# A softmax with a relative bias: the first chunk loaded in two halves, the second half shared unevenly among the DMA engines

## The chip, the cores and the metric

The kernel runs on one core of a Trainium2 chip. The metric is the device time of one execution in microseconds. Three runs of the kernel before gave a median of 1329.82 us (1329.43 to 1330.29). A profile was taken of one execution, and the views quoted here are answers of its trace.

## What is computed

The reference adds a bias to attention logits and takes a softmax over the last axis. The bias depends on the head and on the distance of the two positions, clipped to 16 on either side:

```python
B, H, S, max_rel = 2, 8, 2112, 16
rel = pos[:, None] - pos[None, :]                    # pos = 0 .. S-1
bias = rel_bias[:, clip(rel, -16, 16) + 16]          # rel_bias: (8, 33)
x = logits + bias[None]                              # logits: (2, 8, 2112, 2112) float32
x = exp(x - x.max(-1)); out = x / x.sum(-1)
```

Input and output have 285 MB each, so 571 MB pass through the core; the bias table has 264 numbers.

## The kernel before, in words

The 33,792 rows of 2,112 numbers are dealt out to the 128 partitions: partition p has 264 rows that follow one another in memory, and eight partitions share a head. The work goes in 44 chunks of six rows per partition. A chunk is 128 x 12,672 numbers, 6.49 MB. Four buffers X0 to X3 (`NBUF`) hold chunks; chunk n uses buffer n mod 4, and is loaded, computed on in place, and stored from there.

Before the loop, the bias table is brought to all partitions (line 97, the queue of ScalarE) into the first 264 columns of a tile F, on every partition all eight heads. VectorE makes masks from two index patterns that GpSimd writes (lines 117 to 128), keeps the row of the partition's own head by a multiplication and a sum over heads (lines 131 and 135, into `rbS`), and from it writes a long strip M of bias values into PSUM (lines 138 to 155). For every four chunks (24 rows) the stretch of M that these rows need is copied to F (line 160), so F is used twice: for the table first, then for the strips.

Per chunk, VectorE adds the bias to each row and finds the row's extreme in one instruction (line 166, six to a chunk), ScalarE takes the exponential and its sum (line 175), and VectorE scales by the reciprocal (lines 183 and 187), three rows at a time. Semaphores link them: `ld[b]` tells VectorE that chunk b has landed, `added` and `expd` link VectorE and ScalarE row by row, and `scaled` tells SP that rows are ready to be stored. A wait followed by a decrement is the helper `take` (line 74), and so many waits stand under L74.

All large transfers are issued by SP, in an order written out by hand. First come the loads of the first four chunks: chunk 0 as six transfers of one row per partition (line 88), the other three whole (line 78). Then the loop (line 204): store a chunk once it is scaled (line 82), wait until the store before it has landed (`st[b]`), and load the next chunk into the buffer that this has freed. The last chunk is stored in two halves of three rows. VectorE begins the loop when the first five transfers of chunk 0 have landed (`pre`, line 190), copies the strip, and then waits for `ld[0]`, the sixth.

A transfer of a tile of 128 partitions is cut into 128 packets, one per partition, which 16 DMA engines carry, eight each: a packet is 8,448 B for one row, 25,344 B for three rows, 50,688 B for a whole chunk. Each engine works through its own packets in the order of their issue. A DMA's semaphore rises by 16 in all.

Of the kernel before, what the change touches and what calls it, by code (L numbers as in the profile page):

```python
# [15 lines left out]
def kernel(  # L16
# [6 lines left out]
    nc = tc.nc  # L23
    P = 128
    B, H, S, S2 = logits.shape
    assert S == S2
    MR = 16
    W = 2 * MR + 1
    ROWS = B * H * S // P
    PB = S // ROWS  # L30
    assert ROWS * P == B * H * S and PB * ROWS == S and PB == H == 8
    R = 6
    NBUF = 4
    STEP = R * NBUF
    N = ROWS // R
    HALF = R // 2
    assert ROWS % STEP == 0
    MW = S + ROWS - 1
    FW = S + STEP - 1
    BIG = 3.0e38  # L40

    io = ctx.enter_context(tc.tile_pool(name="io", bufs=1))
    X = [io.tile([P, R * S], FP32, tag=f"X{b}", name=f"X{b}") for b in range(NBUF)]
    F = io.tile([P, FW], FP32, tag="F", name="F")
    rbS = io.tile([P, W], FP32, tag="rbS", name="rbS")
# [3 lines left out]
    ip = io.tile([P, 3, PB], I32, tag="ip", name="ip")  # L49
# [3 lines left out]
    def view(t, offset, dims):  # L53

        return bass.AP(tensor=t.tensor, offset=t.offset + offset, ap=[[list(t.ap[0])[0], P]] + dims)

    def rows(t, j, n):

        return bass.AP(tensor=t.tensor, offset=t.offset + j * S, ap=[[ROWS * S, P], [1, n * S]])

    with tc.tile_critical(no_gpsimd_drain=True):
        ld = [nc.alloc_semaphore(f"ld{b}") for b in range(NBUF)]
# [3 lines left out]
        scaled = nc.alloc_semaphore("scaled")  # L66
        inv = nc.alloc_semaphore("inv")
        rb = nc.alloc_semaphore("rb")
        pre = nc.alloc_semaphore("pre")
        idx = nc.alloc_semaphore("idx")  # L70
        dve = nc.alloc_semaphore("dve")

        def take(eng, sem, n):
            eng.wait_ge(sem, n).then_inc(sem, -n)  # L74


        def load(j, b):
            nc.sync.dma_start(out=X[b][:, :], in_=rows(logits, j, R)).then_inc(ld[b], 16)
# [5 lines left out]
            ).then_inc(st[b], 16)  # L84


        for r in range(R):
            nc.sync.dma_start(
                out=X[0][:, r * S : (r + 1) * S], in_=rows(logits, r, 1)
            ).then_inc(ld[0] if r == R - 1 else pre, 16)  # L90
        for n in range(1, NBUF):
            load(n * R, n)

        rbB = view(F, 0, [[1, H * W]])
        nc.scalar.dma_start(
            out=rbB,
            in_=bass.AP(tensor=rel_bias.tensor, offset=rel_bias.offset, ap=[[0, P], [1, H * W]]),
        ).then_inc(rb, 16)  # L100
        nc.gpsimd.iota(ip[:, 0], pattern=[[0, PB]], base=0, channel_multiplier=1).then_inc(idx, 1)
        nc.gpsimd.iota(ip[:, 2], pattern=[[1, PB]], base=0, channel_multiplier=0).then_inc(idx, 1)  # L102

        v = nc.vector
        done = [0]

        def then(ins):
            done[0] += 1
            ins.then_inc(dve, 1)

        def settle():
            v.wait_ge(dve, done[0])

        SC = H * W
        mask = [F[:, SC + i * PB : SC + (i + 1) * PB] for i in range(9)]
        dp, dh, eq, hm, gt, le, lt, ra, rz = mask
        v.wait_ge(idx, 2)
        then(v.tensor_scalar(out=ip[:, 1], in0=ip[:, 0], scalar1=3, scalar2=7,  # L118
                             op0=ALU.logical_shift_right, op1=ALU.bitwise_and))
# [7 lines left out]
        for m, op in ((eq, ALU.is_equal), (gt, ALU.is_gt), (le, ALU.is_le), (lt, ALU.is_lt)):  # L127
# [4 lines left out]
            out=view(F, 0, [[W, H], [1, W]]), in0=view(F, 0, [[W, H], [1, W]]),  # L132
            in1=view(F, SC + 3 * PB, [[1, H], [0, W]]), op=ALU.mult))
        settle()
        then(v.tensor_reduce(out=rbS[:, :], in_=view(F, 0, [[1, W], [W, H]]),  # L135
                             axis=mybir.AxisListType.X, op=ALU.add))
        settle()
        low, high = rbS[:, W - 1 : W], rbS[:, 0:1]
        then(v.tensor_scalar(out=ra, in0=gt, scalar1=low, scalar2=None, op0=ALU.mult))  # L139
        then(v.tensor_scalar(out=rz, in0=gt, scalar1=low, scalar2=None, op0=ALU.mult))  # L140
        then(v.tensor_tensor(  # L141
            out=view(F, 0, [[W, PB], [1, W]]), in0=view(F, SC + 2 * PB, [[1, PB], [0, W]]),
            in1=view(rbS, W - 1, [[0, PB], [-1, W]]), op=ALU.mult))
# [6 lines left out]
            out=view(M, U, [[ROWS, PB], [1, W]]), in0=view(F, 0, [[W, PB], [1, W]]),  # L150
            in1=view(F, SC + 8 * PB, [[1, PB], [0, W]]), op=ALU.add))
        then(v.tensor_copy(out=view(M, U + W, [[ROWS, PB], [1, ROWS - W]]),  # L152
                           in_=view(F, SC + 7 * PB, [[1, PB], [0, ROWS - W]])))
        then(v.tensor_copy(out=M[:, 0:U], in_=low.to_broadcast([P, U])))  # L154
# [7 lines left out]
        def add(b):  # L162
            take(v, ld[b], 16)
            for r in range(b * R, (b + 1) * R):
                x = X[b][:, (r - b * R) * S : (r - b * R + 1) * S]
                v.tensor_tensor_reduce(  # L166
                    out=x, in0=x, in1=F[:, STEP - 1 - r : STEP - 1 - r + S], scale=-1.0, scalar=BIG,
                    op0=ALU.add, op1=ALU.min, accum_out=nmax[:, r : r + 1],
# [18 lines left out]
                    v.tensor_scalar_mul(out=x, in0=x, scalar1=rec[:, r : r + 1]).then_inc(scaled, 1)  # L187

        v.sem_inc(dve, -done[0])
        take(v, pre, 16 * (R - 1))  # L190
        with nc.Fori(0, ROWS - STEP + 1, STEP, engines=[ENG.DVE]) as j:  # L191
            strip(j)
            take(v, dve, 1)
# [51 lines left out]
```

## Time and profile before

| what | value |
|---|---|
| median of three runs | 1329.82 us (1329.43 to 1330.29) |
| span of the profiled execution | 1327.7 us |
| VectorE busy | 976.6 us (74%) |
| ScalarE busy | 575.2 us (43%) |
| DMA | 571.11 MB, mean 430 GB/s |
| SP's queue (q1) | 13,536 packets, 99.6% of 16 engines' span |
| bias table (q10) | 0.14 MB, lands 6.2 us after its issue |

The profile's span runs from the program's first instruction to its last, and so the profiled execution's own time is known as this span of 1327.7 us; it is 2.1 us below the median of the runs, which are timed as a whole. In the page, busy times are per engine, a digit is a fortieth of the span, and the GB/s are what the 16 DMA engines moved together. A view of windows gives for each stretch its length, the busy time of VectorE (DVE), ScalarE (ACT) and GpSimd (POOL) with the number of instructions, TensorE's clock, the mean busy share of the DMA engines, and GB/s; packets are counted in the window in which they start, so that a share can be over 1. In a timeline a row has start, length, engine, line, operation and operands; a bracket gives the idle time before it and what ended it. An engine's name with a q is its queue of instructions that only issue or wait.

### The profile page before, as it was taken

Reading aid. Unit: us, or ns where it says so; the run is one execution under the profiler, and the core shown is the slowest. Engines: PE = TensorE matmul, PEld = TensorE weight load, DVE = VectorE, ACT = ScalarE, POOL = GpSimd, SP = SyncE. Lnnn points to the kernel's source line nnn. Section 1 sums busy time; section 2 is a strip of 40 time slices with the busy share of each in tenths; the row PEclk is TensorE's granted clock in tenths of the full one; section 3 lists DMA queues with packets and bytes.
Section 4 is the critical chain, followed back from the end, with each engine's and each line's share of the span. In section 5 each row is a group of like instructions: output and inputs, shape, how many; then the busy total and the mean of one; then the engine's idle time right before and its main releaser. Section 6 shows DMA issues by size and latency. Waiting matters only on the chain. (4 is left out here: it accounts for less than half of the span.)

```text
span 1327.7 us, 2454 instructions
## 1 busy us (share of the span) xinstructions
DVE 976.6 (74%) x911; ACT 575.2 (43%) x539; POOL 0.4 (0%) x6
## 2 busy tenths in 40 slices
DVE  6999667777777776687778777677877776687772
ACT  2564333444444343345444333444444343335440
POOL 0000000000000000000000000000000000000000
DMA  9999999999999999999999999999999999999998
GB/s 392 431 428 437 435 420 437 435 434 425 435 437 434 428 435 434 435 429 429 438 438 432 426 438 437 437 425 437 437 437 425 435 440 437 428 432 438 437 426 359
DMA packets 13683, 571.11 MB, mean 430 GB/s; under 512 B 1521, under 2 KB 1649, under 8 KB 1649
## 3 DMA queue, kind: packets, MB, share of 16 engines
q1 hardware_dynamic: 13536, 570.96, 99.6%
q10 hardware_dynamic: 144, 0.14, 0.1%
q14 instruction: 3, 0.02, 0.0%
HBM read 285.61 MB, written 285.47 MB: 430 GB/s over the span
## 5 line engine op out<-in xcount | busy, mean ns | idle before, releaser
L166 DVE CUSTOM_DVE_ANT_0 X<-X,F 128x2112 f32<-128x2112 f32 x264 | 605.2, 2354 | 301.3 <-DVEq L74 301.3
L175 ACT ACTIVATE X<-X,nmax 128x2112 f32<-128x2112 f32 x264 | 541.7, 2052 | 539.3 <-ACTq L74 517.6
L187 DVE TENSOR_SCALAR X<-X,rec 128x2112 f32<-128x2112 f32 x264 | 332.4, 1315 | 13.2
L175 ACT ACT_TABLE_LOAD x11 | 14.1, 1283 | 183.3 <-ACTq L74 183.3
L175 ACT ACTIVATION_READ_ACCUMULATOR X<-X,nmax 128x1 f32 x264 | 49.2, 186 | 0.0
L160 DVE COPY F<-M 128x2135 f32 x11 | 26.1, 2374 | 6.3 <-DVEq L74 6.3
L166 DVE DVE_READ_ACCUMULATOR2_ANT nmax<- 128x1 f32 x264 | 21.7, 82 | 0.0
L183 DVE RECIPROCAL rec<-tot 128x3 f32<-128x3 f32 x88 | 14.9, 170 | 0.0
L131 DVE TENSOR_TENSOR F<-F 128x264 f32<-128x264 f32 x1 | 0.4, 434 | 4.7 <-DMA F<-in_rel_bias_dram 4.7
L152 DVE COPY M<-F 128x1848 f32<-128x1848 f32 x1 | 2.1, 2077 | 0.0
L118 DVE TENSOR_SCALAR ip<-ip 128x8 int32<-128x8 int32 x1 | 0.2, 173 | 1.3 <-POOL ip L102 1.3
L135 DVE TENSOR_REDUCE rbS<-F 128x33 f32<-128x264 f32 x1 | 0.6, 610 | 0.0
L149 DVE TENSOR_TENSOR M<-F 128x264 f32<-128x264 f32 x1 | 0.4, 441 | 0.0
L141 DVE TENSOR_TENSOR F<-F,rbS 128x264 f32<-128x264 f32 x1 | 0.4, 425 | 0.0
L128 DVE TENSOR_SCALAR F<-F 128x8 f32<-128x8 f32 x4 | 0.4, 166 | 0.0
L154 DVE COPY M<-rbS 128x247 f32<-128x247 f32 x1 | 0.4, 408 | 0.0
L139 DVE TENSOR_SCALAR F<-F,rbS 128x8 f32<-128x8 f32 x1 | 0.2, 231 | 0.0
L145 DVE SCALAR_TENSOR_TENSOR F<-F,rbS 128x8 f32<-128x8 f32 x1 | 0.2, 225 | 0.0
L140 DVE TENSOR_SCALAR F<-F,rbS 128x8 f32<-128x8 f32 x1 | 0.2, 222 | 0.0
L146 DVE SCALAR_TENSOR_TENSOR F<-F,rbS 128x8 f32<-128x8 f32 x1 | 0.2, 219 | 0.0
L124 DVE TENSOR_TENSOR F<-ip 128x8 f32<-128x8 int32 x1 | 0.2, 167 | 0.0
L121 DVE TENSOR_TENSOR F<-ip 128x8 f32<-128x8 int32 x1 | 0.2, 166 | 0.0
(9 smaller groups left out, 1.2 us busy)
## 6 DMA issues: line engine op xcount, KB each, us to landing
X<-in_logits_dram SPq DMA_DIRECT2D x43, 6336.0 KB, 44.6
out_dram<-X SPq DMA_DIRECT2D x43, 6336.0 KB, 52.6
X<-in_logits_dram SPq DMA_DIRECT2D x6, 1056.0 KB, 12.1
out_dram<-X SPq DMA_DIRECT2D x2, 3168.0 KB, 21.1
F<-in_rel_bias_dram ACTq DMA_DIRECT2D x1, 132.0 KB, 6.2
```

Of the source, the lines that this page charges most:

```text
L128: then(v.tensor_scalar(out=m, in0=dp, scalar1=0.0, scalar2=None, op0=op))
L131: then(v.tensor_tensor(out=view(F, 0, [[W, H], [1, W]]), in0=view(F, 0, [[W, H], [1, W]]), in1=view(F, SC + 3 * PB, [[1, H], [0, W]]), op= ...
L135: then(v.tensor_reduce(out=rbS[:, :], in_=view(F, 0, [[1, W], [W, H]]), axis=mybir.AxisListType.X, op=ALU.add))
L141: then(v.tensor_tensor(out=view(F, 0, [[W, PB], [1, W]]), in0=view(F, SC + 2 * PB, [[1, PB], [0, W]]), in1=view(rbS, W - 1, [[0, PB], [-1, ...
L149: then(v.tensor_tensor(out=view(M, U, [[ROWS, PB], [1, W]]), in0=view(F, 0, [[W, PB], [1, W]]), in1=view(F, SC + 8 * PB, [[1, PB], [0, W]] ...
L152: then(v.tensor_copy(out=view(M, U + W, [[ROWS, PB], [1, ROWS - W]]), in_=view(F, SC + 7 * PB, [[1, PB], [0, ROWS - W]])))
L154: then(v.tensor_copy(out=M[:, 0:U], in_=low.to_broadcast([P, U])))
L160: v.tensor_copy(out=F[:, :], in_=M[:, bass.ds(ROWS - STEP - j, FW)]).then_inc(dve, 1)
L166: v.tensor_tensor_reduce(out=x, in0=x, in1=F[:, STEP - 1 - r : STEP - 1 - r + S], scale=-1.0, scalar=BIG, op0=ALU.add, op1=ALU.min, accum_ ...
L175: nc.scalar.activation(out=x, in_=x, func=EXP, scale=-1.0, bias=nmax[:, r : r + 1], accum_out=tot[:, r : r + 1],).then_inc(expd, 1)
L183: v.reciprocal(out=rec[:, r0 : r0 + HALF], in_=tot[:, r0 : r0 + HALF]).then_inc(inv, 1)
L187: v.tensor_scalar_mul(out=x, in0=x, scalar1=rec[:, r : r + 1]).then_inc(scaled, 1)
```

## The change

Three things are changed, all of them before the loop; the loop itself is the same.

- Chunk 0 is loaded in two halves of three rows per partition. The first half is one transfer of 128 packets of 25,344 B. The second half is cut by partitions into eight transfers (`FAN`) of 64, 16, 13, 11, 9, 7, 5 and 3 partitions. The 64 are the even partitions, the 16 are every eighth from 1 on; the lanes 3, 5 and 7 of each group of eight are cut in pairs, 13 and 3, 11 and 5, 9 and 7 partitions. If a transfer of k partitions (k of 16 or fewer) goes to the same first k engines, one packet each, the engines carry 11, 11, 11, 10, 10, 9, 9, 8, 8, 7, 7, 6, 6, 5, 5 and 5 of the packets of the second half.
- The bias table is brought to 16 partitions (every eighth) and no longer to all 128. VectorE first fills the 264 columns with zeros; ScalarE's queue waits for that before it issues the transfer. Behind the sum over heads, two 32 x 32 transposes with a copy between them spread a partition's row over its group of eight, and a copy puts it into `rbS`.
- VectorE begins the loop when both `pre` (the first half) and `fan` (seven of the eight transfers) have come; the eighth raises `ld[0]`.

```diff
+    GROUPS = P // 16
+    FAN = [(64, 0, 0, 2), (16, 0, 1, GROUPS)]
+    FAN += [(k, 0, lane, GROUPS) for lane, k in ((3, 13), (5, 11), (7, 9))]
+    FAN += [(16 - k, k, lane, GROUPS) for k, _, lane, _ in FAN[:1:-1]]
...
-        for r in range(R):
-            nc.sync.dma_start(
-                out=X[0][:, r * S : (r + 1) * S], in_=rows(logits, r, 1)
-            ).then_inc(ld[0] if r == R - 1 else pre, 16)
...
-        rbB = view(F, 0, [[1, H * W]])
-        nc.scalar.dma_start(
-            out=rbB,
-            in_=bass.AP(tensor=rel_bias.tensor, offset=rel_bias.offset, ap=[[0, P], [1, H * W]]),
-        ).then_inc(rb, 16)
...
+        then(v.memset(F[:, 0 : H * W], 0.0))
+
+        nc.scalar.wait_ge(dve, 1)
+        nc.scalar.dma_start(
+            out=bass.AP(tensor=F.tensor, offset=F.offset, ap=[[PB * list(F.ap[0])[0], P // PB], [1, H * W]]),
+            in_=bass.AP(
+                tensor=rel_bias.tensor, offset=rel_bias.offset, ap=[[0, P // PB], [1, H * W]]
+            ),
+        ).then_inc(rb, 16)
+        nc.sync.dma_start(out=X[0][:, 0 : HALF * S], in_=rows(logits, 0, HALF)).then_inc(pre, 16)
+        PSX = list(X[0].ap[0])[0]
+        for i, (k, g, lane, step) in enumerate(FAN):
+            p = g * GROUPS + lane
+            nc.sync.dma_start(
+                out=bass.AP(
+                    tensor=X[0].tensor, offset=X[0].offset + p * PSX + HALF * S,
+                    ap=[[step * PSX, k], [1, HALF * S]],
+                ),
+                in_=bass.AP(
+                    tensor=logits.tensor, offset=logits.offset + (p * ROWS + HALF) * S,
+                    ap=[[step * ROWS * S, k], [1, HALF * S]],
+                ),
+            ).then_inc(ld[0] if i == len(FAN) - 1 else fan, 16)
...
+        Q = 32
+        RB, RT, RC, RW = [SC + 9 * PB + 2 * Q * i for i in range(4)]
+        then(v.memset(F[:, RB : RB + 2 * Q], 0.0))
...
-        then(v.tensor_reduce(out=rbS[:, :], in_=view(F, 0, [[1, W], [W, H]]),
+        then(v.tensor_reduce(out=F[:, RB : RB + W], in_=view(F, 0, [[1, W], [W, H]]),
                              axis=mybir.AxisListType.X, op=ALU.add))
+        settle()
+        then(v.transpose(out=F[:, RT : RT + 2 * Q], in_=F[:, RB : RB + 2 * Q]))
+        settle()
+        then(v.tensor_copy(out=view(F, RC, [[Q, 2], [PB, Q // PB], [1, PB]]),
+                           in_=view(F, RT, [[Q, 2], [PB, Q // PB], [0, PB]])))
+        settle()
+        then(v.transpose(out=F[:, RW : RW + 2 * Q], in_=F[:, RC : RC + 2 * Q]))
+        settle()
+        then(v.tensor_copy(out=rbS[:, :], in_=F[:, RW : RW + W]))
...
-        take(v, pre, 16 * (R - 1))
+        take(v, pre, 16)
+        take(v, fan, 16 * (len(FAN) - 1))
```

More of the change, by code (lines that the diff above doesn't have):

```diff
@@ L40 @@
     BIG = 3.0e38
+    GROUPS = P // 16
+    FAN = [(64, 0, 0, 2), (16, 0, 1, GROUPS)]
+    FAN += [(k, 0, lane, GROUPS) for lane, k in ((3, 13), (5, 11), (7, 9))]
+    FAN += [(16 - k, k, lane, GROUPS) for k, _, lane, _ in FAN[:1:-1]]
+    assert sum(k for k, _, _, _ in FAN) == P
     io = ctx.enter_context(tc.tile_pool(name="io", bufs=1))
@@ L68 @@
         rb = nc.alloc_semaphore("rb")
-        pre = nc.alloc_semaphore("pre")
         idx = nc.alloc_semaphore("idx")
         dve = nc.alloc_semaphore("dve")
+        pre = nc.alloc_semaphore("pre")
+        fan = nc.alloc_semaphore("fan")
         def take(eng, sem, n):
@@ L84, in store @@
             ).then_inc(st[b], 16)
-        for r in range(R):
-            nc.sync.dma_start(
-                out=X[0][:, r * S : (r + 1) * S], in_=rows(logits, r, 1)
-            ).then_inc(ld[0] if r == R - 1 else pre, 16)
-        for n in range(1, NBUF):
-            load(n * R, n)
-        rbB = view(F, 0, [[1, H * W]])
-        nc.scalar.dma_start(
-            out=rbB,
-            in_=bass.AP(tensor=rel_bias.tensor, offset=rel_bias.offset, ap=[[0, P], [1, H * W]]),
-        ).then_inc(rb, 16)
-        nc.gpsimd.iota(ip[:, 0], pattern=[[0, PB]], base=0, channel_multiplier=1).then_inc(idx, 1)
-        nc.gpsimd.iota(ip[:, 2], pattern=[[1, PB]], base=0, channel_multiplier=0).then_inc(idx, 1)
         v = nc.vector
@@ L112, in settle @@
             v.wait_ge(dve, done[0])
+        then(v.memset(F[:, 0 : H * W], 0.0))
[20 more added lines that the diff above has]
+            ).then_inc(ld[0] if i == len(FAN) - 1 else fan, 16)
+        for n in range(1, NBUF):
+            load(n * R, n)
+        nc.gpsimd.iota(ip[:, 0], pattern=[[0, PB]], base=0, channel_multiplier=1).then_inc(idx, 1)
+        nc.gpsimd.iota(ip[:, 2], pattern=[[1, PB]], base=0, channel_multiplier=0).then_inc(idx, 1)
         SC = H * W
```

## The prediction

> **What bounds the kernel now.** I read the page's head first (busy shares, the DMA rows, the queues), then the waits, and then the windows at both ends.
>
> ```profile
> span 1327.7 us, 2454 instructions
> DVE 976.6 (74%) x911; ACT 575.2 (43%) x539; POOL 0.4 (0%) x6
> DMA  9999999999999999999999999999999999999998
> GB/s 392 431 428 437 435 420 437 435 434 425 435 437 434 428 435 434 435 429 429 438 438 432 426 438 437 437 425 437 437 437 425 435 440 437 428 432 438 437 426 359
> ...
> q1 hardware_dynamic: 13536, 570.96, 99.6%
> q10 hardware_dynamic: 144, 0.14, 0.1%
> ```
>
> No compute engine is full, but the DMA row is a 9 in all slices but the last. SP's queue carries 570.96 MB and fills 99.6% of 16 engines' time. Only the first slice (392) and the last (359) move clearly less than about 434 GB/s. So the time is the bytes at that rate, plus what is lost at the two ends, plus what single DMA engines lose on the way. The waits say the same:
>
> ```profile
> DVE X L166 <- DVEq L74: 301.3, 41, 8.8
> ...
> SPq L74 <- SPq L74: 1273.1, 87, 36.9
> ```
>
> VectorE waits 41 times for a chunk to land, 301.3 us in all, and SP waits nearly the whole span for stores. A mean over 16 engines hides a late one, though. The windows over the last microseconds show it:
>
> ```profile
> 1319.00:1320.00 1.00, 0.00 (x0) 0.00 (x0) 0.00 (x0) 1.00 1.06 456
> 1320.00:1321.00 1.00, 0.00 (x0) 0.00 (x0) 0.00 (x0) 1.00 0.53 228
> 1321.00:1322.00 1.00, 0.00 (x0) 0.00 (x0) 0.00 (x0) 1.00 0.47 203
> 1322.00:1323.00 1.00, 0.00 (x0) 0.00 (x0) 0.00 (x0) 1.00 0.41 177
> 1323.00:1324.00 1.00, 0.00 (x0) 0.00 (x0) 0.00 (x0) 1.00 0.41 177
> 1324.00:1325.00 1.00, 0.00 (x0) 0.00 (x0) 0.00 (x0) 1.00 0.18 76
> 1325.00:1326.00 1.00, 0.00 (x0) 0.00 (x0) 0.00 (x0) 1.00 0.12 51
> 1326.00:1327.70 1.70, 0.00 (x0) 0.00 (x0) 0.00 (x0) 1.00 0.00 0
> ```
>
> The last two numbers of a row are the mean share of the 16 engines and the bytes of the packets that start in the window. One engine at 434 / 16 = 27.1 GB/s takes 25,344 B / 27.1 GB/s = 0.94 us for a packet of three rows, which is what the last two stores consist of. At 1321 the rate is 203 / 27.1 = 7.5 engines: some nine have finished, near 1320.9, and seven go on. Two packets (51 KB) start after 1325, so the last of them ends near 1326.2. The same number of packets on every engine thus ends 5.3 us apart. From 1321.0 on there are 203 + 177 + 177 + 76 + 51 = 684 KB left, 27 packets of 0.94 us, 1.6 us of all 16 engines: perfect balance would be worth some 3.6 us.
>
> Where the lag comes from is read from SP's timeline, whose loads are issued when the slowest engine has finished a store, and from two long windows:
>
> ```profile
> 156.76 0.35 SPq L78 DMA_DIRECT2D X<-in_logits_dram  x1
> ...
> 549.26 0.35 SPq L78 DMA_DIRECT2D X<-in_logits_dram  x1
> ...
> 1237.05 0.35 SPq L78 DMA_DIRECT2D X<-in_logits_dram  x1
> ```
>
> ```profile
> 65.00:545.00 480.00, 363.24 (x333) 216.99 (x203) 0.00 (x0) 1.00 1.00 432
> 545.00:1265.00 720.00, 531.86 (x489) 315.93 (x297) 0.00 (x0) 1.00 1.00 434
> ```
>
> A round is one load and one store, 13 of them between the first two rows and 23 between the last two: 392.50 / 13 = 30.19 us, then 687.79 / 23 = 29.90 us. The slowest engine loses 13 x 0.29 = 3.8 us in the first stretch, and nothing is lost later (432 against 434 GB/s says it too). So the lag is made by about 550 us and is then carried unchanged to the end. An offset given to an engine at the start should be carried in the same way.
>
> **The change, part by part.** The start decides four of the parts:
>
> ```profile
> 0.92 0.41 ACTq L97 DMA_DIRECT2D F<-in_rel_bias_dram  x1
> 0.97 3.34 SPq L88 DMA_DIRECT2D X<-in_logits_dram  x6
> ...
> 4.36 1.74 SPq L78 DMA_DIRECT2D X<-in_logits_dram  x3
> 7.16 0.43 DVE L131 TENSOR_TENSOR F<-F 128x264 f32<-128x264 f32 x1 [4.69 <-DMA F<-in_rel_bias_dram]
> ...
> 12.06 0.17 DVE L155 COPY M<-rbS 128x16 f32<-128x16 f32 x1
> 18.48 2.38 DVE L160 COPY F<-M 128x2135 f32 x1 [6.26 <-DVEq L74]
> 21.17 2.36 DVE L166 CUSTOM_DVE_ANT_0 X<-X,F 128x2112 f32<-128x2112 f32 x1 [0.31 <-DVEq L74]
> ...
> 43.07 0.34 SPq L82 DMA_DIRECT2D out_dram<-X  x1
> ```
>
> ```profile
> 0.00:2.20 2.20, 0.80 (x7) 0.00 (x0) 0.42 (x6) 1.00 0.02 4
> 2.20:3.00 0.80, 0.26 (x4) 0.00 (x0) 0.00 (x0) 1.00 1.34 213
> 3.00:4.00 1.00, 0.00 (x0) 0.00 (x0) 0.00 (x0) 1.00 0.64 159
> 4.00:5.00 1.00, 0.00 (x0) 0.00 (x0) 0.00 (x0) 1.00 0.80 239
> 5.00:6.00 1.00, 0.00 (x0) 0.00 (x0) 0.00 (x0) 1.00 0.94 321
> 6.00:7.00 1.00, 0.00 (x0) 0.00 (x0) 0.00 (x0) 1.00 0.94 377
> 7.00:8.00 1.00, 0.81 (x2) 0.00 (x0) 0.00 (x0) 1.00 0.98 414
> ```
>
> Bias in 16 packets instead of 128: from 2.2 to 8.0 the engines move 0.8 x 213 + 159 + 239 + 321 + 377 + 414 = 1,680 KB, where 434 GB/s would give 2,517. That is 1.9 us of DMA time; with the 0.14 MB of bias, which q10 carries just then, 2.2 us are lost to the logits. The loss fades when q10's packets end, about when L131 can start. Bounds: no gain, if it is the engines' start and not the bias (then 0.26 us remain for 118 KB less), and 2.2 us. I take the middle, 1.1 us, since rows of 377 and 414 remain after most of the bias has gone and so some of the ramp is not its doing.
>
> Bias behind a memset: ACT now waits for a VectorE fill of 264 columns, priced like L131 (same shape, 0.43 us); its issue moves from 0.92 to about 1.7. The bias should land by 5 or so, not 7.1. Nothing stands behind that wait on ACT until its first exponential.
>
> VectorE's table: one more small fill, two transposes and two copies of 64 or 33 columns, each waiting for the one before; between 0.17 (L155) and 0.43 (L131) each, at most 2.2 us. The chain from L131 to L155 took 12.23 - 7.16 = 5.1, so the table is ready by about 12. It is hidden by the wait of 6.26 us before L160. If that cover were gone, it would delay the first chunk only.
>
> First chunk: six transfers become nine (128 packets of three rows, then 64, 16, 13, 11, 9, 7, 5, 3). Issuing costs 3.34 / 6 = 0.56 us each, so the three later loads are out by 0.97 + 9 x 0.56 + 1.74 = 7.7 instead of 6.1; the first transfer alone holds every engine until 2.2 + 8 x 0.94 = 9.7, so this is nothing. A transfer's own fixed cost: the first five of before, 5.4 MB, were there by 18.48; from 2.2 at 434 GB/s with the 2.2 us lost they need 14.7, so 1.6 us in five, at most 0.3 each. Three more cost between 0 and 0.9 us; I take 0, because the engines were back at 414 GB/s while such transfers followed one another. [...]
>
> The uneven second half: an engine gets 8 + 11 packets at most in the first chunk, 2.2 + 19 x 0.94 = 20.1, with 1.1 of ramp 21.2. VectorE takes the whole chunk before L160, so that copy moves from 18.48 to about 21.3, and the first store from 43.07 to about 46. Behind it four chunks of 6.49 MB are queued, 25.95 MB or 60 us: 18 us of cover. No engine starves, so this costs nothing.
>
> What it does to the end: an engine with 11 packets has three more than its share, +2.8 us; one with 5 has -2.8; the step is 0.94. If nothing else happened, the last engines would end at 1320.9 + 2.8 = 1323.7, instead of 1326.2: -2.5. That needs the lag of 5.3 either to fall on engines that were given less (2.8 before the others, so 1320.9 - 2.8 + 5.3 = 1323.4), or not to arise among engines that are already apart: losses end once they are 5.3 apart, and 11 against 5 packets is 5.6 apart. Both give about the same end. I take it: -2.5 and -1.1, in all **-3.6 us**.
>
> This sum is against the profiled execution, span 1327.7; the median of 1329.82 is 2.1 above the span, and I add the same: 1326.2.
>
> **Rivals.** (1) The balance does not come about: the paired transfers (13 and 3, 11 and 5, 9 and 7) fill all 16 engines evenly, or the last engine to finish is one that keeps eight. The trace of before has only transfers of 128 packets and no engine's number, so nothing in it excludes this. Only the start gains: 1329.8 - 1.1 = 1328.7. [...]
>
> (2) The other side: one of the engines with 11 packets is among the late. It ends at 1320.9 + 2.8 + 5.3 = 1329.0, 2.8 later than now; with the start's gain 1331.5, without it 1332.6. It decides from a lag of more than 2.5 us on such an engine, and seven engines of 16 have that now. What speaks against: the losses ended with distance, and these engines are the last of all from the outset.
>
> [...]
>
> **How the numbers follow.** Forecast 0.52, at 1326.2; its own range is 1324.8 (2.2 at the start, and 0.3 less lag) to 1327.6 (no gain at the start). Rival 1: 0.20. Rival 2: 0.22, of which 0.14 ends above 1332.5 (no gain at the start, or the late engines lose more), 0.08 below. Rival 3: 0.06, nearly all above. About 0.2%, 2.7 us, is what a measurement of this kernel can tell from no change. Faster than 1327.2: 0.52; above 1332.5: 0.20; between: 0.28. The range goes from 1324.8 to 1332.6 and leaves out about 0.05 below and 0.15 above.
>
> **What would show it.** Right: in the last windows the rate falls in steps over less than 4 us instead of 5.3; the time per round is 29.9 from the first rounds on; windows from 3 to 7 near 400 GB/s; L131's copy in the new kernel at about 5; the strip at about 21. Wrong: one or two engines still moving packets 5 us after the others, a round above 30.1 us up to 500 us, or a DMA share under 0.9 between 8 and 25 us.

## The result, and the profile after

The changed kernel takes 1336.71 us (median of five runs, 1336.50 to 1336.79) against 1330.29 us for the kernel before in the same session. The ratio is 1.0050 with a 95% interval of 1.0037 to 1.0062: slower by about 6.4 us, where 3.6 us less had been forecast. The profiled execution has a span of 1334.7 us against 1327.7, 7.0 us more.

The head of the page of the changed kernel, with the same columns as before:

```profile
span 1334.7 us, 2464 instructions
...
GB/s 309 433 431 436 433 431 433 437 433 434 436 431 431 434 437 431 434 436 433 430 434 437 431 436 434 433 430 436 437 430 434 434 436 428 436 437 430 436 434 317
...
q10 hardware_dynamic: 32, 0.02, 0.0%
```

The bias queue has 32 packets instead of 144, the middle of the span moves as much as before, and the first slice has fallen from 392 to 309 GB/s, the last from 359 to 317. The loss is at the two ends. The windows over the first microseconds show both sides of the start:

```profile
0.00:2.20 2.20, 1.01 (x9) 0.00 (x0) 0.42 (x6) 1.00 0.42 104
2.20:3.00 0.80, 0.26 (x4) 0.00 (x0) 0.00 (x0) 1.00 0.79 222
3.00:4.00 1.00, 0.00 (x0) 0.00 (x0) 0.00 (x0) 1.00 0.89 380
4.00:5.00 1.00, 0.00 (x0) 0.00 (x0) 0.00 (x0) 1.00 0.94 406
5.00:6.00 1.00, 0.00 (x0) 0.00 (x0) 0.00 (x0) 1.00 0.98 417
...
8.00:14.00 6.00, 5.66 (x15) 0.00 (x0) 0.00 (x0) 1.00 0.99 418
14.00:22.00 8.00, 0.00 (x0) 0.00 (x0) 0.00 (x0) 1.00 1.27 260
22.00:30.00 8.00, 1.80 (x1) 0.00 (x0) 0.00 (x0) 1.00 0.80 222
```

In the kernel before, the last two windows are these:

```profile
14.00:22.00 8.00, 3.21 (x2) 0.00 (x0) 0.00 (x0) 1.00 1.16 492
22.00:30.00 8.00, 8.00 (x7) 6.34 (x6) 0.00 (x0) 1.00 0.95 412
```

Up to 8 us the engines are ahead: they reach 380 GB/s in the fourth microsecond, where 159 stood before. Then, from 14 to 30 us, they move 260 and 222 GB/s instead of some 434, which leaves (174 + 212) x 8 us = 3.1 MB undone, 7.1 us of all 16 engines. The share column says 1.27 and 0.80 at the same time, 1.03 in the mean: the engines are not idle, their packets take longer. By the rows, 25,344 B take 25,344 B x 1.27 x 16 / 260 GB/s = 1.98 us of an engine from 14 to 22 us and 1.46 from 22 to 30, where the row from 8 to 14 gives 0.96. This is the stage of the small transfers of the second half. Its effect is seen in the timeline, here the instructions that the prediction had placed:

```profile
1.40 0.58 ACTq L106 DMA_DIRECT2D F<-in_rel_bias_dram  x1
1.42 6.22 SPq L116 DMA_DIRECT2D X<-in_logits_dram  x8
...
7.87 0.43 DVE L152 TENSOR_TENSOR F<-F 128x264 f32<-128x264 f32 x1 [5.41 <-DMA F<-in_rel_bias_dram]
...
28.20 2.38 DVE L190 COPY F<-M 128x2135 f32 x1 [14.26 <-DVEq L80]
...
52.78 0.35 SPq L88 DMA_DIRECT2D out_dram<-X  x1
...
89.17 0.36 SPq L84 DMA_DIRECT2D X<-in_logits_dram  x1
...
164.18 0.34 SPq L84 DMA_DIRECT2D X<-in_logits_dram  x1
...
433.29 0.35 SPq L84 DMA_DIRECT2D X<-in_logits_dram  x1
...
1243.76 0.34 SPq L84 DMA_DIRECT2D X<-in_logits_dram  x1
```

The strip begins at 28.20 instead of 18.48. The first load that waits for a store, which the slowest engine decides, is issued at 89.17. In the kernel before it is this row:

```profile
81.12 0.36 SPq L78 DMA_DIRECT2D X<-in_logits_dram  x1
```

So the last engine is 8.05 us late when the start is over. From there to the last load it takes 1243.76 - 89.17 = 1154.59 us, against 1237.05 - 81.12 = 1155.93: 1.3 us are won back. From the last load to the end it is 90.9 against 90.6, 0.3 more. 8.05 - 1.34 + 0.3 = 7.0 us: the difference is accounted for.

The rounds say why something is won and why it is little. Nine rounds from 164.18 to 433.29 take 29.90 us each, the undisturbed time; in the kernel before the 13 rounds from 156.76 to 549.26 took 30.19. But the 27 rounds from 433.29 to 1243.76 take 30.02 each, 3.1 us more than at 29.90. The windows at the end show what that is:

```profile
1322.00:1323.00 1.00, 0.00 (x0) 0.00 (x0) 0.00 (x0) 1.00 1.06 456
1323.00:1324.00 1.00, 0.00 (x0) 0.00 (x0) 0.00 (x0) 1.00 0.82 355
1324.00:1325.00 1.00, 0.00 (x0) 0.00 (x0) 0.00 (x0) 1.00 0.65 279
...
1328.00:1329.00 1.00, 0.00 (x0) 0.00 (x0) 0.00 (x0) 1.00 0.29 127
1329.00:1330.00 1.00, 0.00 (x0) 0.00 (x0) 0.00 (x0) 1.00 0.06 25
...
1332.00:1333.00 1.00, 0.00 (x0) 0.00 (x0) 0.00 (x0) 1.00 0.06 25
```

From 1323 to 1329 the engines finish in steps, as their shares say; then one engine alone (25 KB a microsecond is one packet) works for nearly 4 us.

### The profile page after: what moved, and what is told of

It is laid out like the page before. It is cut to its first block, busy times and chain, and to the rows that moved or that the text cites. A ratio compares the mean times of both kernels' runs of the same rounds, so it can differ in the third digit from the quotient of the medians.

```text
span 1334.7 us, 2464 instructions
## 1 busy us (share of the span) xinstructions
DVE 977.7 (73%) x917; ACT 575.2 (43%) x539; POOL 0.4 (0%) x6
## 5 line engine op out<-in xcount | busy, mean ns | idle before, releaser
L205 ACT ACT_TABLE_LOAD x11 | 14.1, 1283 | 192.2 <-ACTq L80 192.2
```

Source lines behind the costliest of these rows:

```text
L205: nc.scalar.activation(out=x, in_=x, func=EXP, scale=-1.0, bias=nmax[:, r : r + 1], accum_out=tot[:, r : r + 1],).then_inc(expd, 1)
```

## The experiments

Three theories were held against each other. T: the small transfers write partitions that lie eight apart, and because of these partitions their packets take about twice as long (the crowding); the two is the author's estimate, from the 1.98 us above. S: each small transfer has a fixed cost. U: the uneven shares themselves make the end late. Ten more kernels were run, e1 to e10, and the kernel before and the changed kernel once more, each in a session with the kernel before beside it.

**The second half in one transfer (e1).**

```diff
-    FAN = [(64, 0, 0, 2), (16, 0, 1, GROUPS)]
-    FAN += [(k, 0, lane, GROUPS) for lane, k in ((3, 13), (5, 11), (7, 9))]
-    FAN += [(16 - k, k, lane, GROUPS) for k, _, lane, _ in FAN[:1:-1]]
...
+    FAN = [(128, 0, 0, 1)]
...
```

> The second half of chunk 0 is one transfer of 128 partitions, and the bias still goes to 16 partitions; no uneven shares are left. [...] With the start about 2 us ahead (windows from 3 to 8 us near 400 GB/s, as in the changed kernel) the time is 1327.5 to 1329.5; the engines are together again, so the lag of the first 500 us should come back, with a round near 30.2 us. Rival S (each transfer has a fixed cost of about a microsecond): also faster than the changed kernel, by the seven transfers that are gone, some 7 us, so 1328 to 1331. Rival U (the uneven shares, not the slow packets, make the end late): the end is 2.8 us earlier than the changed kernel, 1333 to 1334.

**Even shares, still eight partitions apart (e2).**

```diff
...
+    FAN = [(64, 0, 0, 2)] + [(16, 0, lane, GROUPS) for lane in (1, 3, 5, 7)]
...
```

> The second half in five transfers, 64 partitions and four times 16, each of these eight partitions apart; every engine takes eight packets. Theory T: the four transfers of 16 take 1.9 us a packet instead of 0.94, so 4 x 0.94 = 3.8 us more than the one transfer of 128, and the time is 3 to 5 us over that kernel. Rival S: three or four microseconds less than the changed kernel, as three transfers fewer, but the packets take 0.94 us. Rival U: no loss against one transfer of 128.

**Even shares, 16 neighbouring partitions at a time (e3).**

```diff
...
+    FAN = [(16, 0, 16 * i, 1) for i in range(8)]
...
```

> The second half in eight transfers of 16 partitions that lie side by side; every engine takes eight packets, one of each transfer. [...] Rival S: as many transfers as in the changed kernel and the same time, 1335 to 1338. Rival U: as one transfer of 128, 1327.5 to 1331.

Measured, against the kernel before at 1331.59 in that session: e1 1331.57 us (ratio 1.0001, 0.9992 to 1.0010), e2 1334.72 (1.0026, 1.0016 to 1.0035), e3 1350.50 (1.0147, 1.0132 to 1.0163). The time of e1 lies in none of the three ranges given for it; e2 lies over e1 by what T had expected, e3 by far more than S or U had given it. In e1 the first load that waits for a store is issued where it was before:

```profile
80.85 0.36 SPq L81 DMA_DIRECT2D X<-in_logits_dram  x1
```

Against e1, then, four transfers of 16 that lie eight apart cost 3.15 us, and eight of 16 side by side 18.9 us. The windows of the stage, of e1, e2 and e3:

```profile
14.00:22.00 8.00, 5.82 (x6) 0.70 (x1) 0.00 (x0) 1.00 1.14 494
22.00:30.00 8.00, 8.00 (x7) 7.99 (x8) 0.00 (x0) 1.00 0.95 412
```

```profile
14.00:22.00 8.00, 0.27 (x3) 0.00 (x0) 0.00 (x0) 1.00 1.19 298
```

```profile
14.00:22.00 8.00, 0.13 (x2) 0.00 (x0) 0.00 (x0) 1.00 0.85 101
22.00:30.00 8.00, 0.00 (x0) 0.00 (x0) 0.00 (x0) 1.00 1.09 130
```

What one small transfer takes is read from the view of the line that issues them, first for e2, then for e3:

```profile
L114 SPq DMA_DIRECT2D X<-in_logits_dram x5: 575/589/852, 1.4 to 4.2; - x5
...
DMA to landing us min/median/max: 14.1/16.4/18.6
```

```profile
L114 SPq DMA_DIRECT2D X<-in_logits_dram x8: 412/428/457, 1.4 to 4.7; - x8
...
DMA to landing us min/median/max: 13.6/23.8/33.8
```

If they land in the order of their issue, then in e2 the first transfer (64 partitions) lands at 1.4 + 14.1 = 15.5 and the last at 4.2 + 18.6 = 22.8: 7.3 us for four, 1.8 each, and 4 x 405.5 KB / 7.3 us = 222 GB/s. In e3 it goes from 15.0 to 38.5: 23.5 us for seven, 3.36 each, 121 GB/s. Alone on its engine a packet takes 0.94 us (25,344 B at 434 / 16 GB/s; the share of 0.06 in the last rows of the changed kernel is one such packet in a microsecond). The same 16 packets of the same size, one per engine, take two and three and a half times that, by which partitions they write. That fewer engines carried them does not fit: at full speed the 130 GB/s of e3 would fill 0.30 of the engines, and the share is 1.09. S had given e3 the time of the changed kernel, 1335 to 1338; U had given both the time of e1. Both fall as the cause of the slow stage; that uneven shares add something of their own in the changed kernel is not excluded by this. Why the partitions decide it, no run shows.

**The same rows, without SBUF (e8).** The rows read also differ between e1, e2 and e3, so a kernel copies the rows of lanes 1, 3, 5 and 7 from `logits` to `out` instead, four times 16 packets, behind e1's loads.

```diff
+        for d, lane in enumerate((1, 3, 5, 7)):
+            cut = [[GROUPS * ROWS * S, 16], [1, HALF * S]]
+            nc.sync.dma_start(
+                out=bass.AP(tensor=out.tensor, offset=out.offset + lane * ROWS * S, ap=cut),
+                in_=bass.AP(tensor=logits.tensor, offset=logits.offset + (lane * ROWS + HALF) * S, ap=cut),
+            ).then_inc(fan, 16)
...
```

> The kernel with one transfer of 128 for the second half, and behind it four copies of 16 packets from logits to out, of the partitions' rows eight apart (lanes 1, 3, 5, 7), the rows that the changed kernel loads with its transfers of 16 and fewer. Source rows, packet count and sizes are those of the slow stage, only SBUF is not written; the bytes are overwritten by the stores later. If the crowding is at SBUF (theory T), each copy takes 0.94 us, 3.8 us for the four, and the windows from 18 to 22 us stay near 434 GB/s. If it is the rows in HBM that lie eight partitions apart, or the form of a transfer of 16 packets, each takes about 1.9 us, 7.5 us for the four, and the windows fall to about 215 GB/s.

```profile
L125 SPq DMA_DIRECT2D out_dram<-in_logits_dram x4: 574/589/659, 1.9 to 3.8; - x4
...
DMA to landing us min/median/max: 17.6/18.6/19.2
```

From 1.9 + 17.6 = 19.5 to 3.8 + 19.2 = 23.0 are 3.5 us for three, 1.17 each. That is not quite 0.94, but far from 1.8, and from 18 to 22 us the packets that start make 482 GB/s and not the 215 of the other reading: the rows in HBM and the form of a transfer of 16 packets explain at most 0.23 of the 0.86 us by which a packet in e2 is longer. The time of this kernel, 1333.99 in one run, includes the copies' bytes.

**The bias alone (e4).** The kernel before with the changed bias load, fill and transposes, chunk 0 in six transfers of one row. Against the changed kernel this is

```diff
...
-        for i, (k, g, lane, step) in enumerate(FAN):
...
+        for r in range(R):
+            nc.sync.dma_start(
+                out=X[0][:, r * S : (r + 1) * S], in_=rows(logits, r, 1)
+            ).then_inc(ld[0] if r == R - 1 else pre, 16)
...
```

> The kernel before with one part of the change alone: the bias table goes to 16 partitions, behind the fill, with the transposes; chunk 0 is loaded in six transfers of one row. If the 128 packets of the bias slow the start, the windows from 3 to 7 us rise from 159 to 377 GB/s to near 380 to 410, and the time falls by 1 to 2 us, to 1328 to 1329. If it is the packets of one row that make the start slow, the windows stay as before and the time is within 0.4 us of the kernel before.

The windows of its start:

```profile
3.00:4.00 1.00, 0.00 (x0) 0.00 (x0) 0.00 (x0) 1.00 0.99 406
4.00:5.00 1.00, 0.00 (x0) 0.00 (x0) 0.00 (x0) 1.00 1.05 439
```

406 and 439 instead of 159 and 239: loading the bias to 128 partitions was what slowed the start (its issue also comes 0.5 us later here). By 8 us the logits of e4 are 1.7 us ahead of those of the kernel before. Yet the time is 1332.13, ratio 1.0008 (0.9999 to 1.0017), where 1328 to 1329 had been expected: no gain. On the slowest engine almost nothing was left of it by the first load that waits for a store, which in the kernel before was issued at 81.12:

```profile
81.02 0.36 SPq L77 DMA_DIRECT2D X<-in_logits_dram  x1
```

More was lost later. The ends show it, first of e4, then of the kernel before, profiled again in a later session:

```profile
1319.00:1320.00 1.00, 0.00 (x0) 0.00 (x0) 0.00 (x0) 1.00 0.30 127
...
1326.00:1327.00 1.00, 0.00 (x0) 0.00 (x0) 0.00 (x0) 1.00 0.23 101
...
1329.00:1330.00 1.00, 0.00 (x0) 0.00 (x0) 0.00 (x0) 1.00 0.06 25
```

```profile
1319.00:1320.00 1.00, 0.00 (x0) 0.00 (x0) 0.00 (x0) 1.00 1.06 456
...
1325.00:1326.00 1.00, 0.00 (x0) 0.00 (x0) 0.00 (x0) 1.00 0.18 76
1326.00:1327.00 1.00, 0.00 (x0) 0.00 (x0) 0.00 (x0) 1.00 0.00 0
```

In e4 most engines have finished by 1319, a good microsecond before those of the kernel before, but four go on until 1327 and one to 1330. The engines start together as before and lose time as before (5.3 us on the slowest by 550 us, 4.7 in the kernel before, against rounds of 29.90), and here the late ones lost more: the eleven times of e4 lie 2.4 us apart, and the profiled execution took 1333.70, the longest, so this end is worse than that of the median.

**The kernel before and the changed kernel again.**

> The kernel before, unchanged, profiled on the same chip as the others. Its last engines ended 5.3 us after the first in the first profile, those of the kernel with the quicker start 8 to 10 us. If the lag differs from execution to execution, this profile shows another lag than 5.3 us (6 to 10) and the time varies by 2 to 3 us between runs; if the quicker start makes the larger lag, it is 5.3 us again.

> The changed kernel, unchanged, beside the others: 1336 to 1337.5, with little spread between runs, since its engines are apart from the start and lose nothing by chance; the rate falls again between 16 and 25 us, and a single engine moves packets alone in the last 3 to 4 us.

The kernel before took 1330.20 (1329.22 to 1331.15), and its last packets again start after 1325, as the rows above show: a lag near that of the first profile, not the larger one of e1 and e4. Whether a quicker start makes the lag larger or the sessions differ can't be said from two profiles of one and one of each of the others. The changed kernel took 1336.50 (1336.48 to 1336.71), ratio 1.0042 (1.0029 to 1.0056), as expected: it varies by 0.2 us, the kernel before by 2 in these eleven runs and by 5 in the 21 others of that session.

**Offsets without crowding (e5, e7, e6).** e1 with six copies from `logits` to `out` of 13, 11, 9, 7, 5 and 3 packets, meant to give the first engines 6 and the last none: the uneven shares by themselves, though with extra bytes, three packets an engine in the mean. The packets have three rows (steps of 0.94 us at 434 / 16 GB/s), two (0.63) or one (0.32).

```diff
+        for d, k in enumerate((13, 11, 9, 7, 5, 3)):
+            cut = [[ROWS * S, k], [1, EXTRA * S]]
+            nc.sync.dma_start(
+                out=bass.AP(tensor=out.tensor, offset=out.offset + d * EXTRA * S, ap=cut),
+                in_=bass.AP(tensor=logits.tensor, offset=logits.offset + d * EXTRA * S, ap=cut),
+            ).then_inc(fan, 16)
...
+        take(nc.sync, fan, 16 * 6)
         store(0, 0)
...
```

> The kernel with one transfer of 128 for the second half, and behind it six copies of three rows from logits to out, of 13, 11, 9, 7, 5 and 3 packets. They touch no SBUF and their bytes are overwritten by the stores later; they stand for the uneven shares alone, 6 to 0 packets of 0.94 us on an engine, without the crowding of partitions eight apart. Theory T (offsets are carried to the end and keep engines from losing time where a load turns into a store; only the crowding cost the changed kernel its time): no loss after 65 us (rounds of 29.9 us from the first, 434 GB/s from 65 to 545), the last windows fall in even steps over 5.6 us, and with the first engines at 1320 the last packet ends at 1325 to 1326: time 1326.5 to 1328.5, against 1331.6 without the copies. Rival V (the loss belongs to certain engines, whatever their distance): the late ones lose up to 10 us as before, and with up to 5.6 us of extra packets among them the time is 1333 to 1339.

> As the kernel with six copies of three rows, with copies of two rows: steps of 0.63 us, 3.75 us between the first and the last engine. Theory T: the same with less, the last packet ends at 1323.5 to 1325 if 3.75 us is far enough apart, time 1325 to 1327; if it is not far enough, some engines lose time until they are 5 to 6 us apart and the time is 1327 to 1330. Rival V: 1332 to 1336.

> As the kernel with six copies of three rows, with copies of one row: steps of 0.32 us, 1.9 us between the first and the last engine. Theory T: too near, so the loss comes back in part, a round over 30 us in the first 500 us and a time of 1328 to 1331. Rival V: the time without the copies and up to 1.9 us, 1331 to 1334.

Measured, against the kernel before at 1330.90 in that session: e5 1332.47 (ratio 1.0012, 1.0003 to 1.0021), e7 1331.12 (1.0003, 0.9993 to 1.0012), e6 1329.88 (0.9992, 0.9983 to 1.0001), with little spread (0.4 us over 11 runs for e5, 1.1 for e6, 3.3 for the kernel before). Views of e5:

```profile
65.00:545.00 480.00, 360.80 (x331) 216.60 (x203) 0.00 (x0) 1.00 1.00 434
...
1324.00:1325.00 1.00, 0.00 (x0) 0.00 (x0) 0.00 (x0) 1.00 0.29 127
1325.00:1326.00 1.00, 0.00 (x0) 0.00 (x0) 0.00 (x0) 1.00 0.06 25
...
1328.00:1329.00 1.00, 0.00 (x0) 0.00 (x0) 0.00 (x0) 1.00 0.06 25
```

Hardly any time is lost up to 545 us (434 GB/s, e7 the same), and 15 engines end in steps near 1325, as T expected. In e6, whose engines start at most 1.9 us apart by its packets, an estimate, some of the loss came back (433 GB/s), as T expected too. Rival V, by which the late engines lose up to 10 us whatever their distance, does not fit these first 545 us. What T did not expect is the last row: again one engine alone, for 4 us. That accounts for most of the miss of e5: 1332.47, where 1326.5 to 1328.5 had been expected; e7 has 1331.12 where 1325 to 1327 had been. The uneven shares without the crowding thus cost 1.6 us in e5 and 0.2 in e7, and brought no clear gain. But the copies carry bytes that the changed kernel does not have: 48 packets of 0.94 us on 16 engines are 2.8 us in e5, an estimate. What uneven shares would be worth without them, no run shows.

**Who is the one engine? (e9, e10).** On e1 again: copies of two rows issued by GpSimd, meant to give the high engines five, the first five none (e9), and then the same turned by eight engines (e10). Copies of 128 elements fill each deal up to 16 packets, and in e10 eight more of them stand ahead and behind:

```diff
...
+        for d, k in enumerate((11, 9, 7, 5, 3)):
+            for m, row, n in ((16 - k, ROWS - 1, 128), (k, d * EXTRA, EXTRA * S)):
+                cut = [[ROWS * S, m], [1, n]]
+                at = row * S + (d * 128 if n == 128 else 0)
+                nc.gpsimd.dma_start(
+                    out=bass.AP(tensor=out.tensor, offset=out.offset + at, ap=cut),
+                    in_=bass.AP(tensor=logits.tensor, offset=logits.offset + at, ap=cut),
+                ).then_inc(fan, 16)
...
```

> One transfer of 128 for the second half, and copies of two rows from logits to out that GpSimd issues, each behind a small one, so that the large ones should fall on the engines from 5 on (five packets on the last three, none on the first five). In the kernels with copies on the first engines one engine falls behind by 0.12 us a round up to the end, and ends 3.5 us after the others; by its place it has five of six copies. If it is engine 3 or 4 and starts among the first here, its loss is used up by the offset, the last packet ends near 1324 and the time is 1326.5 to 1328.5. If the loss goes with being late and not with an engine, one of the last three falls behind, and the time is 1330 to 1332. If GpSimd's copies do not fall on the engines as supposed, the windows at the end show no even steps.

> The kernel with GpSimd's copies of two rows, with a small copy of eight packets ahead of the others and another behind them, so that the same shares should fall on engines that are turned by eight: if the engine that falls behind by 0.12 us a round is one certain engine, it has another place now. Where it had four copies (2.9 us behind the first at 79 us), it then has none or nearly none, the last engine ends 4 to 4.5 us after the first, the last packet near 1325, and the time is 1327.5 to 1329. If the loss goes with the place (the fourth or fifth from the end), the same 6.9 us and 1331.2 come out again.

e9 took 1331.24 (ratio 1.0005, 0.9996 to 1.0014) and e10 1331.60 (1.0008, 0.9999 to 1.0017). Neither helped, and both times are near those expected for a loss that goes with the place. In e10's loads the same break is seen, seven rounds of 29.90 us and then 29 of 30.04:

```profile
157.86 0.35 SPq L81 DMA_DIRECT2D X<-in_logits_dram  x1
...
367.18 0.35 SPq L81 DMA_DIRECT2D X<-in_logits_dram  x1
...
1238.35 0.35 SPq L81 DMA_DIRECT2D X<-in_logits_dram  x1
```

So the loss came out again after the shares had been turned, which speaks for a place in the order and against one certain engine; but that GpSimd's copies fell on the engines supposed is not shown, and the cause of this steady loss stays open. No run beat the kernel before clearly; e6, at 0.08% less, is nearest.

## Why the prediction was wrong

The step that failed is the first chunk in nine transfers, priced at 0 (0 to 0.9 us), and with it the uneven second half, where the last engine was to have its 19 packets at 21.2. Each packet was taken at 0.94 us, as in transfers of 128 partitions. The packets of transfers of 16 partitions eight apart took 1.8 us in e2; in the changed kernel the strip began at 28.20 and not at 21.3, and the last engine was 89.17 - 80.85 = 8.3 us behind that of e1, which differs only in this. By e2's price, an estimate, the first engines' seven packets of small transfers take 7 x 1.8 = 12.6 us where e1's four take 4 x 0.94 = 3.8, so 8.8 more: 2.8 for the three extra packets, which the prediction had counted, and 6.0 for the crowding, which it had put at 0. The trace of before had only transfers over all partitions; the bounds were taken from their spacing, and no upper bound looked at which partitions the new transfers write.

Point by point:

- Start with 16 bias packets, -1.1 (0 to 2.2): right in kind, and larger at first. By 8 us the logits were 2.0 us ahead (2,427 - 17 KB against 1,689 - 135 KB), and 1.7 of it came with the bias alone (e4). That the gain reaches the end was assumed and is wrong: on the slowest engine 0.1 us of it was left at 81 us in e4 and 0.3 in e1, and neither kernel was faster. Why the slowest engine had lost it by then is not shown.
- Bias ready by 5: wrong, 7.87. In e4, with packets of one row ahead of it, it is 6.80, so the packets of three rows explain some 1.1 us; the rest is open. Hidden all the same, as said.
- VectorE's table, SP's issues, the late first store: right in that they cost nothing. The first store moved to 52.78 and not to 46, still inside the cover of 60 us of queued loads, and the engines did not starve (436 GB/s from 30 to 65 us).
- Losses end when engines are apart, and offsets are carried: right where the engines start apart, with rounds of 29.90 from some 160 us on for six to nine rounds, in the changed kernel and in e5, e9 and e10. It is no general rule: in e1 and e4, whose engines start together, the slowest engine had lost 5.9 and 5.3 us by 550 us, against rounds of 29.90, and still lost 2.4 and 3.5 us behind that.
- The end at -2.5: wrong by a second thing, the one engine that loses 0.12 us a round until the end. It took 3.1 us in the changed kernel. The trace of before gave rounds of 29.90 to the end. That would fit if the late engines there were others, but its rows name no engine.
- Rivals: (3), with its 0.06 nearly all above 1332.5, stood for a fixed cost of each small transfer, with engines idling in between; that the time lies there is luck. No run shows such a cost: with as many transfers as the changed kernel e3 took 18.9 us more than e1, the changed kernel 6.4 us more than the kernel before, whose time e1 has; the copies of 16 packets in e8 took at most 0.23 us more than 0.94 each, and what the small transfers of e2 and e3 showed in its place is 1.8 and 3.36 us a packet at shares of 1.19 and 1.09. (1) did not come about: rounds of 29.90 us from 164 us on and the steps at the end from 1323 to 1329 fit uneven shares, though no row names an engine. (2) came about in part: an engine that was not the last at the start fell behind by 3.1 us, but whether it was one with 11 packets is not shown. The price of crowding was in none of them.

The sum that the trace shows in its place, at the engine that ends last: +8.05 until the first load that waits for a store (the crowding and the extra packets, 8.3 us against e1, less the 0.3 that the start had gained there), -1.34 over the rounds (the losses of engines in step avoided, less the 3.1 us of the one engine), +0.3 at the end, 7.0 us in all.

## What to carry to other kernels

A transfer's rate depended here on which partitions it wrote, not only on its bytes and its number of packets (1.8 us a packet in e2, 3.36 in e3, 0.94 in a full tile): before cutting one by partitions, see that those in flight together spread as a full tile does, and take the price from a row in which such a set of partitions is written. A gain at the start counted here only as far as the engine that ends last had it (e4: 1.7 us at 8 us, 0.1 at 81 us, no gain in time); look at the windows of the last microseconds before promising it. Engines that started apart lost less time on the way here than engines in step (0.4 us over the 13 rounds from 164.18 to 553.31 in the changed kernel, 3.8 over the 13 up to 549.26 in the kernel before, against rounds of 29.90), but the offset had to be paid for at the end, which fell in steps from 1323 to 1329 us.

## What the runs showed of the hardware

- A transfer of 16 packets of 25,344 B takes 1.8 us into partitions eight apart (e2) and 3.36 us into 16 neighbouring ones (e3), in the mean of such transfers behind one another; in a full tile a packet takes 0.94 us, an estimate from 434 GB/s.
- 128 packets of 1,056 B beside the first loads held the engines to 159 and 239 GB/s in the fourth and fifth microsecond; with 16 such packets it is 406 and 439 (e4).
- Engines that started in step lost time in the first 550 us (rounds of 30.2 to 30.3 us in both profiles of the kernel before and in e1 to e4); engines that start 3 to 6 us apart, by their extra packets, which is an estimate, hardly did (rounds of 29.90 from 158 to 164 us on in e5, e9, e10 and the changed kernel, 434 GB/s from 65 to 545 us in e7).
- In the changed kernel, e5, e9 and e10 the rounds grow from 29.90 to about 30.02 us after six to nine of them, counted from 158 to 164 us on, and in the changed kernel and e5 one engine works alone for the last 4 us or nearly: about 0.12 us are lost a round. The cause is not known.
